# The last two rows of products: one fixed order on TensorE, neighbours in different two-bank tiles, and the last half product in a bank of its own

## The chip, the cores and the metric

The kernel runs on one core of a Trainium2 chip. The metric is device time in microseconds (us); lower is better. The core has five engines that run side by side, each through its own queue in order: TensorE (PE in the profile, with PEld for its weight loads), VectorE (DVE), ScalarE (ACT), GpSimd (POOL) and SyncE (SP), which here only issues transfers. Matrix products land in PSUM, an accumulator memory of eight banks of 128 partitions x 512 float32; everything else that an engine works on lies in SBUF.

## The reference

One layer of a transformer-like block on 512 tokens of 2048 features, in float32:

```python
h = rmsnorm(x, g_attn[l])
proj = h @ w_in[l]                       # q, k, v of 8 + 8 heads, and the forget gates
o_sb, o_fox = stick_breaking_attention(...), forgetting_attention(...)
x = x + concat(head_rmsnorm(o_sb), head_rmsnorm(o_fox)) @ w_out[l]
h2 = rmsnorm(x, g_mlp[l])
u = relu(h2 @ w_up[l])                   # 8192 columns
x = x + (u * u) @ w_down[l]
...
return rmsnorm(x, g_final)               # y, 512 x 2048
```

The change lies wholly in the last two lines: the last part of the product with `w_down`, and the final rmsnorm that needs the sum of squares of a whole row of 2048 values before any of that row can be written.

## The kernel before

Every matrix is split into a high and a low part, and a product is three matmuls (`mm3`, lines 104 to 106: high x high, high x low, low x high). The big products are formed by Strassen-like sums of seven. The product with `w_down` runs over 8192 hidden columns in groups; all but the last four blocks of 128 hidden columns go through the seven-product scheme. The last four blocks are multiplied plainly, by `last_product(t, n, ps)`: `t` is one of four blocks of 128 tokens ("row" t0 to t3), `n` one of four blocks of 512 output columns (n0 to n3). A product (t, n) is 12 matmuls of 128x512 into one PSUM bank: four blocks of hidden columns, three matmuls each. In this document "t2 n3" is such a product. The very last, t3 n3, is made in two halves of 256 columns, which this document calls half a and half b.

After a product, `last_product` issues three more steps. L1240: VectorE adds the PSUM bank onto the running sum `x2(t, n)` in SBUF. L1242: ScalarE squares the result and sums it along the row into `ss3` (two instructions: ACTIVATE and the reading of its accumulator). L1244: GpSimd multiplies the sum by the gain `gf` in place. For the two halves of t3 n3, VectorE does that multiplication itself, into `last_piece` (L1246).

When a row is complete, `last_row(t)` makes the factor of the rmsnorm and scales and stores the row. For t2: L1254 and L1255 (VectorE, mean of the squares), L1265 and L1266 (ScalarE, logarithm and exponential), L1267 and L1268 (VectorE, a Newton step), two scalings of 128x1024 on VectorE (L1276) and two stores (L1277), the first from SyncE's queue and the second from ScalarE's queue. For t3: `mean_square` for the first three squares ahead (L1254, L1255), then L1263 and L1264 once the halves are squared, the same L1265 to L1268, four scalings on VectorE and ScalarE (L1280 to L1284) and four stores (L1286).

PSUM at this stage holds four tiles of two banks each, taken in turn by `two_banks(i)` from three pools: `mps`, `mps2` and two buffers of `dps`. Rows t0 and t1 take one tile for each `n`, with t0 in its first bank and t1 in its second. Rows t2 and t3 take one tile for two neighbouring `n` of the same row: t2 n0 and n1 in one tile, t2 n2 and n3 in the next, t3 n0 and n1, and t3 n2 and n3 in the last. Dependencies between the engines are kept by tile: the first matmul into one bank of a tile waits for VectorE's reading of the other bank if that reading was issued earlier in the program.

In most of the kernel the order on TensorE, ScalarE and VectorE is written out by hand. In this last stage it is not: a scheduler orders the instructions of each engine by its own estimate of times, and `tc.issue_after(ins)` is the means to hold it: instructions of an engine issued inside that block are placed behind `ins` on that engine's queue. It adds no semaphore. In the kernel before, the products of rows t2 and t3 carry no such tie, and the scheduler has put them on TensorE in this order (matmuls in brackets), from t2 n1 on:

```
t2n1 (12)  t2n2 (1)  t1n3 (12)  t2n2 (11)  t3n0 (12)  t3n2 (11)  t2n3 (12)  t3n1 (12)  t3n2 (1)  t3n3 a (12 halves)  t3n3 b (12 halves)
```

Of the kernel before, what the change touches and what calls it, by code (L numbers as in the profile page):

```python
# [16 lines left out]
TB = NT // P  # L17
# [18 lines left out]
def block_kernel(ctx, tc, x, g_attn, w_in, b_f, g_out_sb, g_out_fox, w_out, g_mlp, w_up, w_down, g_final, y):  # L36
# [66 lines left out]
    def mm3(out, sh, sl, mh, ml, first, last):  # L103
        pe.matmul(out, sh, mh, start=first, stop=False, skip_group_check=True)  # L104
        pe.matmul(out, sh, ml, start=False, stop=False, skip_group_check=True)  # L105
        return pe.matmul(out, sl, mh, start=False, stop=last, skip_group_check=True)  # L106
# [59 lines left out]
    with tc.tile_pool(name="att", bufs=1, side="right", reuse_waits="tile") as at:  # L166
# [15 lines left out]
        def accumulate_v(c0, m, steps, prepare=None, more=None, pool_=None):  # L182

            per = NT // m
            banks = [(acc if pool_ is None else pool_).tile([P, NT], F32, tag="acc", name="accv")
                     for _ in range(2 if more is not None else TB // per)]
            if more is not None:
                banks += [more.tile([P, NT], F32, tag="more", name="accm") for _ in range(2)]
            ps = [banks[t // per][:, t % per * m:(t % per + 1) * m] for t in range(TB)]
            k1 = 0  # L190
            for step in steps:
                k0, k1 = k1, k1 + step
                if prepare is not None:
                    prepare(k0, step)
                w = load_w([w_in[k0 * P:(k0 + step) * P, c:c + m // len(c0)].rearrange("(a p) c -> p a c", p=P) for c in c0],
                           step, m)
                for t in range(TB):
                    ts = slice(t * P, (t + 1) * P)
                    for i in range(step):
                        k = k0 + i  # L200
                        mm3(ps[t], hH[k][:, ts], hL[k][:, ts], *w[i], k == 0 and t % per == 0, k == KC - 1)
            return ps
# [126 lines left out]
        def v_columns(h):  # L329
            return 2 * WSB + h * P if h < NH else o0 + 2 * WSB + (h - NH) * P  # L330

        with tc.tile_pool(name="tr0", bufs=2, space=PSUM) as trp:
# [36 lines left out]
            ps = accumulate_v([v_columns(order[0])], 2 * P + NH, [1, 1] + [2] * 7, prepare, trp)  # L369
# [25 lines left out]
        with tc.tile_pool(name="attp", bufs=1, space=PSUM, reuse_waits="tile") as atp:  # L395
# [54 lines left out]
            for n in range(0, 2 * NH, 2):  # L450
# [15 lines left out]
                if n == 2 * NH - 2:  # L466
                    ps = accumulate_v([v_columns(order[n])], 2 * P, [4] * 4, pool_=accs[1])
# [228 lines left out]
    def out_piece(p, db, m0):  # L696

        hi, lo = (w.rearrange("p (a b) -> p a b", a=2) for w in hi_lo(2 * NT))
        if db == 0 and p in (1, 2):
            begun_ = [sp.dma_start(w.bitcast(F32), wraws[p - 1][:, m0 // 2, i]) for i, w in enumerate((hi, lo))][1]  # L700
        elif db == 0 and p == 6:
            begun_ = sp.dma_start(hi.bitcast(F32), whigh[:, m0 // 2])
            sp.dma_start(lo.bitcast(F32), wsums[:, m0 // 2, 3, db])
        else:
            raw = out_weights(p, db, m0)
            casts[0] = split(hi, lo, raw[0])
            begun_ = raw[1]
        ps = {2: B[db], 5: C, 3: C}.get(p, A[db])
        for t in range(2):
            ts = slice(t * P, (t + 1) * P)  # L710
            for i in range(2):
                mm3(ps[:, t, :], G[p][0][:, m0 + i, ts], G[p][1][:, m0 + i, ts], hi[:, i, :], lo[:, i, :],
                    m0 + i == 4 and p in (1, 5, 2), m0 + i == 3)
        return begun_
# [60 lines left out]
    for db in range(2):  # L775
# [25 lines left out]
        for i, p in enumerate(G_ORDER):  # L801
            for m0 in (2,) if db == 0 and p in (1, 2) else (4, 6, 0, 2):
                ins = out_piece(p, db, m0)
# [96 lines left out]
    def x2(t, n):  # L900
        return M[QUADS[t // 2][n // 2]][:, t % 2, n % 2, :]
# [78 lines left out]
    ins = units[0].multiply(1, begun[0])  # L980
# [5 lines left out]
    for p in (1, 2):  # L986
        ins = units[1].product(p)
    left_form(4, 1, 0)
    left_form(5, 1, 0)
    for p in (5, 6, 7, 4, 3):  # L990
        for j in range(2):

            with tc.issue_after(ins.ins):
                ins = units[j].product(p)
# [80 lines left out]
    with tc.manual_schedule(engines={pe.engine, act.engine, dve.engine}):  # L1075
# [5 lines left out]
        for k in range(len(steps)):  # L1081
            n = steps[k][2]
# [45 lines left out]
    ws, us = {}, [None, None]  # L1128
# [28 lines left out]
    bs, srcs, rooms, banks, residual = {(0, 0): b_first}, {}, {}, {}, []  # L1157

    def down_at(k):
        g, db, i, p, u0 = down[k]  # L1160
        return g, db, i, p, u0, min(2, GROUPS[g][1] - u0)

    with tc.manual_schedule(engines={pe.engine, act.engine, dve.engine}):
        for k in range(-4, len(down)):
            g, db, i, p, u0, m = down_at(max(k, 0))
# [35 lines left out]
            n = GROUPS[g][1]  # L1201
# [7 lines left out]
    g, db, i, p = down[-1][:4]  # L1209
# [15 lines left out]
        for o, a, b_ in sums:  # L1225
            dve.tensor_tensor(*(M1[db] if i == 1 else M[i][:, :, db, :] for i in (o, a, b_)), op=ALU.add)

    def last_product(t, n, ps):
        ts = slice(t * P, (t + 1) * P)

        parts = [slice(0, NT)] if (t, n) != (TB - 1, 3) else [slice(0, 2 * P), slice(2 * P, NT)]
        for j, cols in enumerate(parts):
            for i in range(4):
                wh, wl = ws[n, i // 2]
                mm3(ps[:, cols], *(h[:, ts] for h in us[i // 2][i % 2]), wh[:, i % 2, cols], wl[:, i % 2, cols],
                    i == 0 and j == 0, i == 3)
        order_ = ExitStack()
        for j, cols in enumerate(parts):
            x2_ = x2(t, n)[:, cols]
            ins = dve.tensor_tensor(x2_, x2_, ps[:, cols], op=ALU.add)  # L1240
            junk = spare.tile([P, NT], F32, tag="junk", name="junk3")
            act.activation(junk[:, cols], x2_, AF.Square, accum_out=last_sum if j else ss3[:, t, n:n + 1])  # L1242
            if len(parts) == 1:
                pool.tensor_tensor(x2_, x2_, gf[:, n * NT:(n + 1) * NT], op=ALU.mult)  # L1244
            else:
                scaled = dve.tensor_tensor(last_piece[:, cols], x2_, gf[:, n * NT:(n + 1) * NT][:, cols], op=ALU.mult)  # L1246
                order_.enter_context(tc.issue_after(scaled.ins))
        order_.close()
        return ins

    def mean_square(t, tile):

        v, c = tile, 4 if t < TB - 1 else 3
        dve.tensor_reduce(v, ss3[:, t, :c], axis=mybir.AxisListType.X, op=ALU.add)  # L1254
        dve.tensor_scalar(v, v, 1.0 / D, ev[:, t:t + 1], op0=ALU.mult, op1=ALU.add)  # L1255

    def last_row(t):

        v, a, b_ = (cp.tile([P, 1], F32, name=f"{c}3{t}") for c in "vab")
        if t < TB - 1:  # L1260
            mean_square(t, v)
        else:
            dve.tensor_scalar(before_last, ss3[:, t, 3:4], 1.0 / D, before_last, op0=ALU.mult, op1=ALU.add)  # L1263
            dve.tensor_scalar(v, last_sum, 1.0 / D, before_last, op0=ALU.mult, op1=ALU.add)  # L1264
        act.activation(a, v, AF.Ln)  # L1265
        act.activation(a, a, AF.Exp, scale=-0.5)  # L1266
        dve.tensor_scalar(b_, a, v, a, op0=ALU.mult, op1=ALU.mult)  # L1267
        dve.tensor_scalar(v, b_, -3.0, a, op0=ALU.add, op1=ALU.mult)  # L1268
        rows_ = y[t * P:(t + 1) * P]
        if t < TB - 1:  # L1270
            for i, q in enumerate((sp, act)):
                m = M[QUADS[t // 2][i]][:, t % 2]
                if t < 2:
                    act.mul(m, m, v)
                else:
                    dve.tensor_scalar(m, m, v, None, op0=ALU.mult)  # L1276
                q.dma_start(rows_[:, i * 2 * NT:(i + 1) * 2 * NT].rearrange("p (a b) -> p a b", a=2), m)  # L1277
        else:
            m = [x2(t, 0), x2(t, 1), x2(t, 2), last_piece]
            act.mul(m[1], m[1], v)  # L1280
            dve.tensor_scalar(m[3], m[3], v, None, op0=ALU.mult)
            dve.tensor_scalar(m[0], m[0], v, None, op0=ALU.mult)
            act.mul(m[2][:, 2 * P:], m[2][:, 2 * P:], v)
            dve.tensor_scalar(m[2][:, :2 * P], m[2][:, :2 * P], v, None, op0=ALU.mult)  # L1284
            for n, q in ((3, sp), (1, act), (0, sp), (2, act)):
                q.dma_start(rows_[:, n * NT:(n + 1) * NT], m[n])  # L1286
# [18 lines left out]
    def two_banks(i):  # L1305
        return homes[i][0].tile([P, 2, NT], F32, tag=homes[i][1], name="acce")

    for n in range(4):
        two = two_banks(n)
        for t in range(2):  # L1310
            last_product(t, n, two[:, t])
    for db in range(2):
        closing(db, (7, 7, 6), (4, 4, 7), (7, 7, 5))
    for t in range(2):
        last_row(t)
    for t in range(2, TB):
        for n in range(4):
            if n % 2 == 0:
                two = two_banks(2 * (t - 2) + n // 2)
            ins = last_product(t, n, two[:, n % 2])  # L1320
            if (t, n) == (TB - 1, 2):
                mean_square(t, before_last)
        with tc.issue_after(ins.ins):
            last_row(t)
# [29 lines left out]
```

## Time and profile before

| what | value |
|---|---|
| median of 3 runs | 2051.01 us (2050.29 to 2051.45) |
| the profiled execution's own time | 2051.27 us |
| span of the profiled execution, first to last instruction | 2049.5 us |
| granted TensorE clock, mean | 0.999 |
| TensorE busy | 2030.9 us, 99% of the span |
| VectorE / ScalarE / GpSimd busy | 1667.6 / 1093.2 / 57.9 us |
| last matmul of 128x512 starts / last matmul of all ends | 2035.5 / 2040.2 us |

Times in the profile are microseconds from the start of the span. A timeline row gives start, duration, engine, line, operation, output and inputs, shapes, how often; in square brackets stands how long the engine was idle before it and which instruction released it. Consecutive instructions of an engine overlap at their edges, by some tenths of a microsecond. A row of the chain of work that ended last gives the start of a piece, its share of the chain in us, and the instruction.

### The profile page before, as it was taken

What the parts mean: (1) busy time and instruction counts of PE and PEld (TensorE: products, weight loads), DVE (VectorE), ACT (ScalarE), POOL (GpSimd) and SP (SyncE); (2) the same over time, 40 slices, a digit from 0 to 9 for tenths busy, and PEclk for the clock granted to TensorE, in tenths of its full rate; (3) what the DMA queues carried; (4) which work ended last, traced back from release to release, by engine and by line L of the source; (5) the groups of instructions that cost most, each with busy time, mean ns of one, the idle gap of its engine ahead of it and who ended that gap; (6) DMA issues with size and microseconds to landing.
All of it is one profiled execution on the core that took longest, in us unless ns stands there. A gap on an engine that the chain in (4) does not pass through costs nothing.

```text
span 2049.5 us, 26810 instructions
## 1 busy us (share of the span) xinstructions
PE 2030.9 (99%) x10322; PEld 1735.9 (85%) x10322; DVE 1667.6 (81%) x1892; ACT 1093.2 (53%) x1578; POOL 57.9 (3%) x76
## 2 busy tenths in 40 slices
PE   8999999999999999999999999999999999999997
PEld 8888888888888888988888888888888888888886
DVE  5677755566577678899999999998798888888896
ACT  5444433445455566667677676776644344444443
POOL 0000000000010000000000000000000000000004
PEclk9999999999999999999999999999999999999999
DMA  7878743232328882656666667667685674674642
GB/s 242 292 289 269 254 127 90 73 93 75 80 74 276 281 279 90 221 175 190 212 195 208 200 196 221 186 205 256 231 298 202 224 259 171 233 264 170 218 152 82
DMA packets 258848, 402.40 MB, mean 196 GB/s; under 512 B 9456, under 2 KB 154912, under 8 KB 251168
## 3 DMA queue, kind: packets, MB, share of 16 engines
q1 hardware_dynamic: 257760, 398.56, 58.8%
q10 hardware_dynamic: 960, 2.13, 0.3%
q8 instruction: 81, 1.33, 0.3%
q14 instruction: 47, 0.39, 0.1%
HBM read 307.85 MB, written 92.80 MB: 195 GB/s over the span
## 4 chain that ended last, share of the span: by engine, by line
PE 94%; DVE 3%; ACT 1%; DMA 1%; issue 1%; SPq 0%; POOL 0%; ACTq 0%; DVEq 0%
PE psa L594 10%; PE accd L104 8%; PE accd L106 8%; PE accd L105 8%; PE accq L105 6%; PE accq L104 6%; PE accq L106 6%; PE psa L596 5%; PE psc L594 5%; PE psc L596 3%; PE psb L594 3%; PE accv L104 2%; PE accv L105 2%; PE accv L106 2%; PE m L104 1%; PE m L105 1%
## 5 line engine op out<-in xcount | busy, mean ns | idle before, releaser
L1172 ACT CAST wh<-wd 128x1024 fp32r<-128x1024 f32 x126 | 125.0, 999 | 166.3 <-PE accd L106 54.8
L1062 DVE TENSOR_TENSOR wl<-wu,wh 128x1024 fp32r<-128x1024 f32 x157 | 191.4, 1220 | 15.3 <-ACT wh L1056 15.3
L104 PE MATMUL accq<-hH,wh 128*128 128x512 f32 x512 | 200.6, 392 | 0.4 <-DVE vl L75 0.4
L106 PE MATMUL accq<-hH,wl 128*128 128x512 f32 x512 | 200.4, 391 | 0.0
L105 PE MATMUL accq<-hL,wh 128*128 128x512 f32 x512 | 200.3, 391 | 0.0
L594 PE MATMUL psa<-f,wh 128*128 128x512 f32 x728 | 182.5, 393 | 0.3 <-ACT l L628 0.3
L1056 ACT CAST wh<-wu 128x1024 fp32r<-128x1024 f32 x157 | 166.4, 1060 | 28.5 <-issue 11.3
L105 PE MATMUL accd<-wl,uf 128*128 128x512 f32 x436 | 169.8, 389 | 0.0
L106 PE MATMUL accd<-wh,uf 128*128 128x512 f32 x436 | 169.8, 389 | 0.0
L104 PE MATMUL accd<-wh,uf 128*128 128x512 f32 x436 | 169.6, 389 | 0.0
L72 DVE TENSOR_TENSOR wl<-wraw,wh 128x1024 fp32r<-128x1024 f32 (+2 forms) x101 | 119.7, 1186 | 56.5 <-ACT wh L71 50.9
L71 ACT CAST wh<-wraw 128x1024 fp32r<-128x1024 f32 (+2 forms) x101 | 101.8, 1009 | 112.8 <-PE accq L105 69.2
L1179 DVE TENSOR_TENSOR wl<-wd,wh 128x1024 fp32r<-128x1024 f32 x126 | 144.0, 1151 | 13.2 <-ACT wh L1172 12.7
L594 PEld LDWEIGHTS psa<-f,wh 128*128 128x128 f32 x728 | 131.1, 189 | 23.9 <-ACT l L628 0.5
L946 DVE TENSOR_TENSOR m<-m,accd 128x1024 f32<-128x1024 f32 x84 | 102.2, 1217 | 47.7 <-PE accd L106 47.7
L1172 ACT CAST wx<-wd 128x1024 fp32r<-128x1024 f32 (+1 forms) x82 | 80.8, 994 | 110.6 <-PE accd L106 43.6
L104 PEld LDWEIGHTS accq<-hH,wh 128*128 128x128 f32 x512 | 96.2, 188 | 20.1 <-PE accv L106 0.8
L106 PEld LDWEIGHTS accq<-hH,wl 128*128 128x128 f32 x512 | 96.2, 188 | 19.3
L105 PEld LDWEIGHTS accq<-hL,wh 128*128 128x128 f32 x512 | 96.2, 188 | 19.2
L104 PE MATMUL accd<-wx,uf 128*128 128x512 f32 x284 | 110.6, 389 | 0.0
L105 PE MATMUL accd<-wx,uf 128*128 128x512 f32 x284 | 110.6, 389 | 0.0
L106 PE MATMUL accd<-wx,uf 128*128 128x512 f32 x284 | 110.6, 389 | 0.0
(375 smaller groups left out, 4933.0 us busy)
## 6 DMA issues: line engine op xcount, KB each, us to landing
wu<-in_w_up_dram SPq DMA_DIRECT2D x60, 1024.0 KB, 6.5
ufd<-st SPq DMA_DIRECT2D x98, 512.0 KB, 3.9
wd<-in_w_down_dram SPq DMA_DIRECT2D x48, 1024.0 KB, 7.8
wraw<-in_w_in_dram SPq DMA_DIRECT2D x84, 512.0 KB, 3.8
uf<-ufd SPq DMA_DIRECT2D x42, 1024.0 KB, 6.9
mixed<-in_w_out_dram SPq DMA_DIRECT2D x8, 2048.0 KB, 7.7
wsums<-mixed SPq DMA_DIRECT2D x8, 2048.0 KB, 7.3
wo<-wsums SPq DMA_DIRECT2D x28, 512.0 KB, 4.4
```

Source lines behind the costliest of these rows:

```text
L71: ins = act.copy(hi, src)
L72: lows[0] = dve.tensor_tensor(lo, src, hi.bitcast(F32), op=ALU.subtract)
L104: pe.matmul(out, sh, mh, start=first, stop=False, skip_group_check=True)
L105: pe.matmul(out, sh, ml, start=False, stop=False, skip_group_check=True)
L106: return pe.matmul(out, sl, mh, start=False, stop=last, skip_group_check=True)
L594: pe.matmul(ps, hi[:, a, :], f_both(p, a), start=a == PAIRS[0] and p in (1, 5), stop=False, skip_group_check=True)
L596: ins = pe.matmul(ps[:, 2 * P:], lo[:, a, :], f_parts(p, a)[0], start=False, stop=a == PAIRS[-1], skip_group_check=True)
L946: dve.tensor_tensor(M[p][:, :, db, :], M[p][:, :, db, :], ps, op=ALU.add)
L1056: act.copy(rooms[k][0], srcs[k])
L1062: lows[0] = dve.tensor_tensor(lo, srcs.pop(k), hi.bitcast(F32), op=ALU.subtract)
L1172: act.copy(rooms[k + 3][0], srcs[k + 3])
L1179: dve.tensor_tensor(rooms[k + 2][1], srcs.pop(k + 2), rooms[k + 2][0].bitcast(F32), op=ALU.subtract)
```

## The change

It does three things, all in the code for rows t2 and t3.

First, the four PSUM tiles are now taken once, when t = 2, one for each `n`, and shared by the two rows: t2 n in the first bank of tile n, t3 n in the second. Two products that follow each other on TensorE thus lie in different tiles.

Second, the matmuls of each product are placed behind the last matmul of the product before, in the order of the program.

Third, half b of t3 n3 no longer lies in the bank of half a. It goes into the first bank of tile 1, where t2 n1 was. Each half now begins its own accumulation.

```diff
-    def last_product(t, n, ps):
+    def last_product(t, n, *banks):
...
-        for j, cols in enumerate(parts):
+        for ps, cols in zip(banks, parts):
             for i in range(4):
                 wh, wl = ws[n, i // 2]
-                mm3(ps[:, cols], *(h[:, ts] for h in us[i // 2][i % 2]), wh[:, i % 2, cols], wl[:, i % 2, cols],
-                    i == 0 and j == 0, i == 3)
+                mul = mm3(ps[:, cols], *(h[:, ts] for h in us[i // 2][i % 2]), wh[:, i % 2, cols], wl[:, i % 2, cols],
+                          i == 0, i == 3)
         order_ = ExitStack()
-        for j, cols in enumerate(parts):
+        for j, (ps, cols) in enumerate(zip(banks, parts)):
...
-        return ins
+        return mul, ins
...
+    four, mul = [], None
     for t in range(2, TB):
         for n in range(4):
-            if n % 2 == 0:
-                two = two_banks(2 * (t - 2) + n // 2)
-            ins = last_product(t, n, two[:, n % 2])
+            if t == 2:
+                four.append(two_banks(n))
+            banks = [four[n][:, t - 2]] + ([four[1][:, 0]] if (t, n) == (TB - 1, 3) else [])
+            with ExitStack() as order_:
+                if mul is not None:
+                    order_.enter_context(tc.issue_after(mul.ins))
+                mul, ins = last_product(t, n, *banks)
```

The built program differs from the one before only in this stage. The number of instructions is the same on every engine. TensorE's order from t2 n1 on becomes:

```
t2n1 (12)  t1n3 (12)  t2n2 (12)  t2n3 (12)  t3n0 (12)  t3n1 (12)  t3n2 (12)  t3n3 a (12 halves)  t3n3 b (12 halves)
```

VectorE's order, from the addition of t2 n3 on, in the kernel before (upper line, from t3 n0) and after:

```
before: add t3n0, add t2n3, L1254 L1255 L1267 (t2), add t3n1, add t3n2, L1268 (t2), L1276 x2, L1254 L1255 (t3), add a, L1246 a, add b, L1263, L1246 b, L1264 ...
after:  add t2n3, L1254 L1255 L1267 (t2), add t3n0, L1268 (t2), L1276 x2, add t3n1, add t3n2, add a, L1254 (t3), L1246 a, L1255 (t3), add b, L1263, L1246 b, L1264 ...
```

On ScalarE the squares follow those additions; the store of t2's second half (L1277), which waits for the second L1276, stands ahead of the square of t3 n1 in the kernel after, and behind the square of t3 n2 in the kernel before. ScalarE's other L1277 stores move behind one square each. The orders of GpSimd and SyncE are the same.

## The prediction

> **What bounds the kernel now.** I read the page first (busy shares and the chain that ended last), then the chain from 2032 us on, then each engine's timeline of the last 35 us.
>
> ```profile
> PE 2030.9 (99%) x10322; PEld 1735.9 (85%) x10322; DVE 1667.6 (81%) x1892; ACT 1093.2 (53%) x1578; POOL 57.9 (3%) x76
> ...
> PE 94%; DVE 3%; ACT 1%; DMA 1%; issue 1%; SPq 0%; POOL 0%; ACTq 0%; DVEq 0%
> ```
>
> TensorE is the bound, and the edit adds and removes no matmul. What can move is an idle gap of TensorE in the last stage, and what follows its last matmul.
>
> ```profile
> 2016.71 0.39 PE L104 MATMUL acce<-ws,us 128*128 128x512 f32 x1
> ...
> 2035.29 0.61 PE L106 MATMUL acce<-ws,us 128*128 128x512 f32 x2
> 2037.08 0.39 PE L104 MATMUL acce<-ws,us 128*128 128x256 f32 x1 [1.17 <-DVE m L1240]
> 2037.30 0.28 PE L105 MATMUL acce<-ws,us 128*128 128x256 f32 x1
> ...
> 2039.94 0.28 PE L106 MATMUL acce<-ws,us 128*128 128x256 f32 x1
> ```
>
> The first row is the first matmul of t2 n1; the last of the pair at 2035.29, starting at 2035.51, is the 84th behind it and the last of 512 columns. Between them TensorE never waits: 18.80 us / 83 steps = 0.2266 us a step, 2.72 us a product. Then it stands idle for 1.17 us: half a of t3 n3 waits for VectorE's addition of t3 n2, which lies in the same two-bank tile and whose last matmul the scheduler had put directly ahead. The 24 half-width matmuls step by 2.64 us / 22 = 0.120 us and end at 2040.22.
>
> ```profile
> 2033.00 0.70 DVE m L1240
> ...
> 2034.48 0.72 ACT junk L1242 x2
> ...
> 2035.84 1.19 DVE m L1240 x2
> ...
> 2037.26 3.55 DVE m L1276 x2
> ...
> 2040.91 0.21 DVE ss L1255
> 2041.12 0.34 DVE m L1240
> ...
> 2041.90 0.34 DVE m L1240
> ...
> 2042.33 0.52 ACT junk L1242 x2
> ...
> 2044.21 0.72 ACT m L1280
> 2044.93 0.40 ACT m L1283
> ```
>
> The chain leaves TensorE even before that gap: at 2033.00 VectorE adds t2 n3, then come t2's mean and factor, two additions, and the two scalings of row t2 (L1276, 3.55 us, to 2040.81). Only then does VectorE reach the halves of t3 n3, although TensorE was done at 2040.22. The addition of half b ends at 2042.24. From there to the end nothing of the edit plays a part. So two things stand in the way: the gap, and row t2's scalings behind t2 n3, a product multiplied late (after t3 n0 and most of t3 n2).
>
> **The change part by part.** I use the program's order on each engine and the steps above.
>
> (1) TensorE's order and tiles. From t2 n1 at 2016.71 the products start 2.72 us apart: t1 n3 2019.43, t2 n2 2022.15, t2 n3 2024.87, t3 n0 2027.59, t3 n1 2030.31, t3 n2 2033.03, half a 2035.74. An addition on VectorE starts 0.20 us after the next product's start:
>
> ```profile
> 2027.79 0.69 DVE L1240 TENSOR_TENSOR m<-m,acce 128x512 f32<-128x512 f32 x1 [1.41 <-PE acce L106]
> 2026.48 2.17 ACT L1274 ACTIVATE m<-m,v 128x1024 f32<-128x1024 f32 x2
> 2033.72 0.63 ACT L1242 ACTIVATE junk<-m 128x512 f32<-128x512 f32 x1 [5.07 <-DVE m L1240]
> 2034.26 0.18 ACT L1242 ACTIVATION_READ_ACCUMULATOR junk<-m 128x1 f32 x1
> 2034.52 2.52 POOL L1244 TENSOR_TENSOR m<-m,gf 128x512 f32<-128x512 f32 x2 [5.17 <-ACT junk L1242]
> 2044.55 0.48 DVE L1282 TENSOR_SCALAR m<-m,v 128x512 f32<-128x512 f32 x1
> 2044.95 0.35 DVE L1284 TENSOR_SCALAR m<-m,v 128x256 f32<-128x256 f32 x1
> ```
>
> (The first row is t3 n0 before, which ended in the place that t2 n3 has now.) Now the waits of the new tiles. t2 n3 takes the tile of t1 n3: added by 2023.3, needed at 2024.87. t3 n2 shares with t2 n2, added by 2025.8, needed at 2033.03. Half a shares with t2 n3, added by 2028.5, needed at 2035.74: the gap goes, with 7 us to spare. The ties themselves cost nothing: they are places in TensorE's own queue and TensorE had no gap between products. So half a starts at 2035.74, the last matmul at 2035.74 + 23 x 0.120 = 2038.50, and TensorE ends at 2038.78, 1.44 us earlier.
>
> (2) Half b in another tile. It waits for the addition of t3 n1, its tile's other bank, which stands behind the L1276 pair on VectorE. Needed at 2037.18, so I follow row t2. Add t2 n3 2027.79 to 2028.48; ScalarE is busy with L1274 until 2028.65, so the square runs 2028.68 to 2029.40 (0.63 + 0.18, overlapping). From L1254 to the first L1276 it took 2034.48 to 2037.26, 2.78 us, with two additions between; with one (0.6 less) L1276 starts at about 2031.6. GpSimd's part for t2 n3 is over by then (2029.5 + 1.26 = 2030.7). The pair takes between 2 x 0.75 us alone (0.48 for 512, 0.35 for 256 columns: 0.13 per 256, so 0.74 for 1024) and the 3.55 it took beside GpSimd: it ends at 2033.1 to 2035.2, I take 2034.3, since one GpSimd operation (t3 n0) falls beside it and two did before. The addition of t3 n1 ends 0.69 later, 2035.0 (at most 2035.9). Half b finds its bank free. The second bank also lets half a be added while half b is multiplied: before, both additions ran after the last matmul.
>
> (3) The moved store. t2's second store now stands ahead of the square of t3 n1 on ScalarE. Its issue took 0.34 us:
>
> ```profile
> 2040.84 0.34 ACTq L1277 DMA_DIRECT2D out_dram<-m  x1
> 2044.96 0.85 ACTq L1286 DMA_DIRECT2D out_dram<-m  x2
> ...
> out_dram<-m ACTq DMA_DIRECT2D x3, 512.0 KB, 2.7
> ```
>
> It waits for the pair, as the addition of t3 n1 does, and is issued beside that addition: nothing is lost. The other moved ScalarE stores are 0.4 us each in a stage where ScalarE idles; SyncE's and GpSimd's queues keep their order, and t2's stores now go some 6 us earlier and land in 2.7, clear of the last ones.
>
> (4) What is late next. Add t3 n2: 2035.94 to 2036.63, square to 2037.38, GpSimd's t3 n2 from 2037.46 (0.08 after, as at 2034.52) to 2038.72. VectorE: add half a at 2037.07 + 0.28 + 0.04 = 2037.39 to 2037.80, L1254, then L1246 on half a, ready at 2038.0, beside GpSimd. What that does is seen here:
>
> ```profile
> 2003.36 1.22 DVE L1226 TENSOR_TENSOR m<-m,m 128x1024 f32<-128x1024 f32 x1
> 2005.06 3.53 POOL L1244 TENSOR_TENSOR m<-m,gf 128x512 f32<-128x512 f32 x2 [3.30 <-ACT junk L1242]
> 2007.36 2.30 DVE L1226 TENSOR_TENSOR m<-m,m 128x1024 f32<-128x1024 f32 x1
> ...
> 2037.26 2.99 POOL L1244 TENSOR_TENSOR m<-m,gf 128x512 f32<-128x512 f32 x2 [0.22 <-ACT junk L1242]
> ...
> 2041.48 0.42 DVE L1246 TENSOR_TENSOR last<-m,gf 128x256 f32<-128x256 f32 x1
> ```
>
> L1226, of two SBUF operands like L1246, took 1.22 us alone and 2.30 when GpSimd worked until 2008.59: it ended 1.07 after GpSimd, so all but 0.15 of it came after. L1246 then ends at 2038.72 + 0.42 - 0.15 = 2038.99, L1255 0.21 later, and the addition of half b (0.34 on the chain) at 2039.54. The bounds: unhindered, L1246 ends at 2038.4, the addition starts 0.04 after TensorE's end and ends at 2038.82 + 0.41 = 2039.23; with the pair at its full 3.55 us, t3 n1's square ends at 2036.7, GpSimd does t3 n1 and n2 one behind the other (2 x 1.26, and 0.25 each as in the 2.99 row) to 2039.7 and half b is added by 2040.5. The rows lie nearest the middle value.
>
> A rule speaks here. The Trainium skill, "SBUF — State Buffer", section "Who interferes with whom", says that VectorE with two SBUF inputs and GpSimd reading SBUF take a shared port in turn and that the second "fully blocks". By it L1246 would run whole behind GpSimd, to 2039.14, and the saving would be 2.55 instead of 2.70 us. The 2.30 row agrees within 0.15 us.
>
> Sum: half b's addition ends at 2039.54 instead of 2042.24, 2.70 us earlier; square, L1264 to L1268, scalings and stores follow at the same distances. The profiled run took 2051.27 us (span 2049.5, 1.77 around it): 2048.57. It stands 0.26 above the median of 2051.01, so against the median 2048.3. The case's own range is 1.7 to 3.0 us saved, 2048.0 to 2049.3, and some 0.6 for the spread of runs (2050.29 to 2051.45) on either side.
>
> **The rivals.** *Only the gap is won.* If VectorE still reaches half b as late after TensorE's end as now (2042.24 - 2040.22 = 2.02 us; forecast 0.76), the saving is TensorE's 1.44 us: 2049.6. For it: L1276 or GpSimd work that falls later than I place it. Against: the pair starts 5.7 us earlier.
>
> *Slower: the L1276 pair holds half b.* Half b waits for an addition queued behind row t2's scalings, a wait that the kernel before did not have. From the pair's end through add, square, two GpSimd operations, L1246 and half b's addition it is 0.69 + 0.75 + 0.08 + 2.52 + 0.27 + 0.55 = 4.9 us; the saving is gone when the pair ends after 2037.4, and the kernel is over 0.2% (4.1 us) slower after 2041.5: 2055.2. That needs t2's factor 6 us later than worked out, for instance ScalarE held by a store that waits for an earlier one to land (2.7 us each). Against: t2's mean needs one square, and ScalarE is free from 2028.65.
>
> *It does nothing.* If the end hung on the last stores alone: 2051.0. Against: they are issued at 2044.96, when L1283 is nearly through, and earlier stores have landed.
>
> *Faster by over 0.2%.* 1.4 us more than the sum, 2046.9 or less: the last stores, now alone in the queues, would have to land sooner as well. Their burst already starts at once; little speaks for it.
>
> **How the numbers follow.** Case by the sum (2048.3) 0.78; only the gap (2049.6) 0.08; nothing (2051.0) 0.04; slower (2055.2) 0.04; faster (2046.9) 0.06. 0.2% is 4.1 us, about what a measurement of this kernel can tell from no change: faster takes the last case and a little of the first's lower edge, 0.1; slower 0.05; within 0.2% the rest, 0.85. The range goes from 2047.2 (3.0 saved, and runs low) to 2050.6, which takes in the gap-only case with the runs' spread.
>
> **What the profile would show.** Right: no idle time of TensorE before the first 256-column matmul; last matmul ending near 2038.8; L1276 near 2031.6, before the addition of t3 n1; half b added by 2039.5; GpSimd's t3 n2 ending just before L1246. Wrong: a wait on L1240 at the first matmul of half b, a chain through L1276 again, or GpSimd's two last operations back to back after 2036.5.

## The result and the profile after

The changed kernel takes 2048.24 us (median of 22 runs, 2047.04 to 2049.67) where the kernel before takes 2050.94 (22 runs, 2049.46 to 2053.24): 2.70 us less. The ratio is 0.9987, with a 95% interval of 0.9981 to 0.9993. So the gain is clear of no change, though it is smaller than the 0.2% at which the prediction drew its line.

The page of the changed kernel, busy shares and the chain that ended last:

```profile
PE 2030.4 (99%) x10322; PEld 1734.8 (85%) x10322; DVE 1666.6 (81%) x1892; ACT 1093.2 (53%) x1578; POOL 57.5 (3%) x76
...
PE 94%; DVE 4%; ACT 1%; issue 1%; DMA 1%; POOL 0%; SPq 0%; ACTq 0%; DVEq 0%
```

The shares say nothing new, as is to be expected when 2.7 us of 2050 are at stake. The profiled execution has a span of 2045.7 us, 3.8 less than that of before, and 2.7 of these are the stage's. To see this, both traces need a common mark. Up to the matmuls of t1 n2 the two programs are the same, so VectorE's addition of t1 n2 serves; in the kernel before:

```profile
2016.91 0.69 DVE L1240 TENSOR_TENSOR m<-m,acce 128x512 f32<-128x512 f32 x1 [2.03 <-PE acce L106]
```

and VectorE's timeline of the changed kernel, with its rows of this stage that matter:

```profile
2015.76 0.69 DVE L1240 TENSOR_TENSOR m<-m,acce 128x512 f32<-128x512 f32 x1 [2.03 <-PE acce L106]
...
2030.28 2.45 DVE L1276 TENSOR_SCALAR m<-m,v 128x1024 f32<-128x1024 f32 x2
2032.65 0.68 DVE L1240 TENSOR_TENSOR m<-m,acce 128x512 f32<-128x512 f32 x1
...
2036.69 1.27 DVE L1246 TENSOR_TENSOR last<-m,gf 128x256 f32<-128x256 f32 x1
...
2038.01 0.41 DVE L1240 TENSOR_TENSOR m<-m,acce 128x256 f32<-128x256 f32 x1
```

The mark lies at 2016.91 and at 2015.76: this execution was 1.15 us ahead before the change could act. From here on, times "after the mark" are times less that of the mark in the same trace. From the mark to the end of the span it is 2049.5 - 2016.91 = 32.59 us before and 2045.7 - 2015.76 = 29.94 us after: 2.65 us less, and this agrees with the medians. TensorE and GpSimd in the changed kernel:

```profile
2034.60 0.28 PE L104 MATMUL acce<-ws,us 128*128 128x256 f32 x1
...
2037.35 0.28 PE L106 MATMUL acce<-ws,us 128*128 128x256 f32 x1
```

```profile
2036.38 1.29 POOL L1244 TENSOR_TENSOR m<-m,gf 128x512 f32<-128x512 f32 x1 [0.88 <-ACT junk L1242]
```

The first half-width matmul has no idle time in front of it any more (before: 1.17 us). Row t2's two scalings start 14.52 us after the mark instead of 20.35, and take 2.45 us instead of 3.55. And the chain that ended last, which left TensorE ahead of the gap before, now follows TensorE through half a of t3 n3, and then half a's gain beside GpSimd:

```profile
2036.23 0.42 DVE m L1240
...
2036.72 1.24 DVE last L1246
2037.96 0.12 DVE ss L1255
2038.08 0.34 DVE m L1240
...
2038.51 0.52 ACT junk L1242 x2
...
2040.38 0.72 ACT m L1280
2041.11 0.40 ACT m L1283
```

The tail behind half b's addition is as long as before: from 2038.42 to 2045.7 it is 7.28 us, before from 2042.24 to 2049.5 7.26.

### The profile page after: what moved, and what is told of

Its sections match the earlier page's. It is cut to its first block, busy times and chain, and to the rows that moved or that the text cites. A ratio compares the mean times of both kernels' runs of the same rounds, so it can differ in the third digit from the quotient of the medians.

```text
span 2045.7 us, 26813 instructions
## 1 busy us (share of the span) xinstructions
PE 2030.4 (99%) x10322; PEld 1734.8 (85%) x10322; DVE 1666.6 (81%) x1892; ACT 1093.2 (53%) x1578; POOL 57.5 (3%) x76
## 4 chain that ended last, share of the span: by engine, by line
PE 94%; DVE 4%; ACT 1%; issue 1%; DMA 1%; POOL 0%; SPq 0%; ACTq 0%; DVEq 0%
PE psa L594 10%; PE accd L104 8%; PE accd L105 8%; PE accd L106 8%; PE accq L104 6%; PE accq L105 6%; PE accq L106 6%; PE psa L596 5%; PE psc L594 5%; PE psc L596 3%; PE psb L594 3%; PE accv L104 2%; PE accv L105 2%; PE accv L106 2%; PE m L104 1%; PE m L105 1%
```

## The experiments

The medians of single kernels here are of 10 or 11 runs each and carry an interval of some 0.09% (1.8 us) on either side, too wide for terms of 0.3 us. The time from the mark to the span's end is free of what happens ahead of the stage. In a second profile of the changed kernel it came out within 0.02 us; every other kernel was profiled once. So each verdict below rests on that time ("the stage"), and the ratio is given beside it.

| kernel | stage, us | against before | TensorE ends | half b added | ratio of medians, 95% interval |
|---|---|---|---|---|---|
| before | 32.59 | | 23.31 | 25.32 | |
| changed | 29.94 | -2.65 | 21.87 | 22.66 | 0.9987 (0.9981 to 0.9993) |
| changed, once more | 29.96 | -2.63 | 21.87 | 22.66 | 0.9986 (0.9977 to 0.9994) |
| ties alone | 33.65 | +1.06 | 25.07 | 26.31 | 1.0007 (0.9998 to 1.0016) |
| tiles and half b's bank alone | 30.79 | -1.80 | 21.87 | 23.42 | 0.9992 (0.9984 to 1.0001) |
| changed, both halves in one bank | 30.45 | -2.14 | 21.87 | 23.11 | 0.9987 (0.9978 to 0.9996) |
| before, t3 n3 in another tile | 32.38 | -0.21 | 21.87 | 25.05 | 1.0000 (0.9991 to 1.0009) |
| changed, halves' gains behind half b | 29.67 | -2.92 | 21.88 | 22.33 | 0.9986 (0.9977 to 0.9995) |
| changed, no gain of t3 n2 | 29.63 | -2.96 | 21.87 | 22.33 | 0.9989 (0.9980 to 0.9997) |
| changed, 4 more scalings | 30.54 | -2.05 | 21.87 | 22.90 | 0.9991 (0.9982 to 1.0000) |
| changed, wait before half a put back | 30.66 | -1.93 | 22.92 | 23.37 | 0.9990 (0.9981 to 1.0000) |
| changed, 8 more scalings | 33.24 | +0.65 | 25.20 | 25.66 | 1.0003 (0.9993 to 1.0012) |

The columns "TensorE ends" and "half b added" are times after the mark; the latter is the end of that addition's row.

### The order alone

```diff
...
-            banks = [four[n][:, t - 2]] + ([four[1][:, 0]] if (t, n) == (TB - 1, 3) else [])
+            if n % 2 == 0:
+                two = two_banks(2 * (t - 2) + n // 2)
...
-                mul, ins = last_product(t, n, *banks)
+                mul, ins = last_product(t, n, *[two[:, n % 2]] * 2)
```

> The products of rows t2 and t3 in one fixed order, but with the old tiles (two neighbours n of one row share a tile) and both halves of t3 n3 in one bank. Theory (the order brings row t2's scalings forward, and the separate tiles take away one wait per pair): three neighbours now follow each other in one tile (t2 n2 and n3, t3 n0 and n1, t3 n2 and n3), each costing TensorE about 1.0 us of idle time (an addition of 0.69 us plus its start, less the step of 0.23). TensorE ends some 2.9 us later than in the changed kernel, the additions of the halves run after it, and the addition of half b ends about 0.6 us later than in the kernel before: 0.3 to 1.0 us slower than before. Rival (the ties alone carry the gain): 1.3 to 2.7 us faster than before.

1.06 us slower in the stage, a little more than the 0.3 to 1.0 expected: TensorE ends 3.20 us later than in the changed kernel, where 2.9 was expected. TensorE's timeline, all its rows of the stage with idle time:

```profile
2027.45 0.50 PE L104 MATMUL acce<-ws,us 128*128 128x512 f32 x1 [0.78 <-DVE m L1240]
2033.96 0.50 PE L104 MATMUL acce<-ws,us 128*128 128x512 f32 x1 [0.78 <-DVE m L1240]
2040.48 0.39 PE L104 MATMUL acce<-ws,us 128*128 128x256 f32 x1 [0.78 <-DVE m L1240]
```

One wait per pair of neighbours, as the theory has it, and the rival falls. Half a starts 21.93 us after the mark against 18.84 in the changed kernel, so a wait costs 1.03 us. The order is no gain of its own. It is paid for with three waits unless the neighbours lie in different tiles. The scheduler's mixed order in the kernel before had only one such wait, of 1.17 us.

### The tiles alone

```diff
-            with ExitStack() as order_:
-                if mul is not None:
-                    order_.enter_context(tc.issue_after(mul.ins))
-                mul, ins = last_product(t, n, *banks)
+            mul, ins = last_product(t, n, *banks)
```

> The new tiles and the separate bank for half b, but no ties: the scheduler then puts t2 n3 one product (12 matmuls, 2.72 us) later on TensorE than the changed kernel does, with t3 n0 ahead of it. Theory: no idle time of TensorE before half a, but row t2's scalings start about 2.7 us later than in the changed kernel, t3 n2's addition waits behind them, and half b is added 0.8 to 1.2 us later: 1.4 to 1.9 us faster than before, where the full change gives 2.7. Rival (tiles alone do it): the full 2.7 us.

1.80 us faster than before, as expected, and 0.85 short of the full change. TensorE ends where it ends in the changed kernel. VectorE's timeline shows what is missing:

```profile
2034.87 2.66 DVE L1276 TENSOR_SCALAR m<-m,v 128x1024 f32<-128x1024 f32 x2
...
2039.05 1.52 DVE L1246 TENSOR_TENSOR last<-m,gf 128x256 f32<-128x256 f32 x1
```

The scalings start 17.26 us after the mark (2034.87 - 2017.61) instead of 14.52: 2.74 us later, one product of 2.72, because without ties the scheduler puts t3 n0 ahead of t2 n3. The additions of t3 n1 and n2 follow the scalings, GpSimd comes to t3 n2 later, and half a's gain beside it ends 22.96 us after the mark instead of 22.20. So the ties are worth 0.85 us, once the tiles are there.

### Half b's bank

```diff
-            banks = [four[n][:, t - 2]] + ([four[1][:, 0]] if (t, n) == (TB - 1, 3) else [])
+            banks = [four[n][:, t - 2]] * 2
...
-                          i == 0, i == 3)
+                          i == 0 and j == 0, i == 3)
```

> The changed kernel with half b back in the bank of half a. Theory: TensorE as in the changed kernel, but the addition of half a waits for the last matmul of half b, so that half a's addition, its gain (0.42 us) and half b's addition stand one behind the other after TensorE's end: half b is added 1.1 us after 38.8 on the scale of the prediction, 0.4 us later than in the changed kernel: 2.3 us faster than before. Rival (the separate bank is what counts): most of the 2.7 us is gone.

2.14 us faster than before, where 2.3 was expected; the separate bank is worth 0.51 us, a fifth of the gain and not most of it, as the rival had it. Half a's addition waits for the last matmul of half b:

```profile
2038.56 0.42 DVE L1240 TENSOR_TENSOR m<-m,acce 128x256 f32<-128x256 f32 x1 [0.93 <-PE acce L106]
2039.01 0.43 DVE L1246 TENSOR_TENSOR last<-m,gf 128x256 f32<-128x256 f32 x1
2039.35 0.41 DVE L1240 TENSOR_TENSOR m<-m,acce 128x256 f32<-128x256 f32 x1
```

### The gap alone, in the old order

```diff
-            ins = last_product(t, n, two[:, n % 2])
+                if (t, n) == (2, 2):
+                    other = two
+            ins = last_product(t, n, two[:, n % 2] if (t, n) != (TB - 1, 3) else other[:, 0])
```

> The kernel before, with t3 n3 alone moved to another tile (that of t2 n2 and n3), in the old order. TensorE's idle 1.2 us before half a goes and TensorE ends 1.4 us earlier. Theory: nothing is gained (0 to 0.2 us), because row t2's scalings still stand in front of the halves' additions on VectorE, ending where they ended. Rival (only the gap is won): 1.4 us faster.

TensorE ends 1.44 us earlier, and the stage is only 0.21 us shorter, as expected. VectorE's timeline:

```profile
2038.17 3.52 DVE L1276 TENSOR_SCALAR m<-m,v 128x1024 f32<-128x1024 f32 x2
2041.61 0.14 DVE L1254 TENSOR_REDUCE ss<-ss 128x1 f32<-128x3 f32 x1
2041.67 0.40 DVE L1240 TENSOR_TENSOR m<-m,acce 128x256 f32<-128x256 f32 x1
```

The scalings end where they ended before (23.87 us after the mark, before 23.90), and half a's addition stands behind them. TensorE's idle time, the wait that catches the eye, was not what set the end.

### The gap alone, in the new order

```diff
-            banks = [four[n][:, t - 2]] + ([four[1][:, 0]] if (t, n) == (TB - 1, 3) else [])
+            banks = [four[n][:, t - 2]] if (t, n) != (TB - 1, 3) else [four[2][:, 0], four[1][:, 0]]
```

Half b's matmuls are tied behind half a's as well, so that the scheduler keeps the halves' order.

> The changed kernel with half a of t3 n3 put back beside t3 n2, into the first bank of its tile, so that the wait for t3 n2's addition returns; order, ties and half b's bank as in the changed kernel. Theory: TensorE waits 1.0 us before half a, as each of the three pairs did with the ties alone, and here it reaches the end: half b is added 0.7 to 0.9 us later than in the changed kernel (0.3 of the 1.0 is hidden behind half a's gain and GpSimd), 1.8 to 2.0 us faster than before. Rival (the gap is worth as little as in the old order): 0.2 us.

```profile
2037.63 0.39 PE L104 MATMUL acce<-ws,us 128*128 128x256 f32 x1 [0.78 <-DVE m L1243]
```

The wait is back with the 0.78 us of the ties alone. TensorE ends 1.05 us later and the stage is 0.72 us longer than in the changed kernel, both as expected. So the wait before half a is worth 0.21 us behind the scalings (1.17 us of idle time) and 0.72 where they are out of the way (0.78 us).

### Half a's gain and GpSimd

Two kernels ask what the new chain hangs on. In the first, the two gains (L1246) leave `last_product` and stand behind the addition of half b:

```diff
-                scaled = dve.tensor_tensor(last_piece[:, cols], x2_, gf[:, n * NT:(n + 1) * NT][:, cols], op=ALU.mult)
-                order_.enter_context(tc.issue_after(scaled.ins))
...
+            scaled = gain(slice(0, 2 * P))
+            with tc.issue_after(scaled.ins):
+                ins = dve.tensor_scalar(v, last_sum, 1.0 / D, before_last, op0=ALU.mult, op1=ALU.add)
+            with tc.issue_after(ins.ins):
+                gain(slice(2 * P, NT))
```

> The changed kernel with the gains of the two halves (the multiplications into last_piece) moved behind the addition of half b: half a's gain just ahead of the row's mean, half b's behind it, in the time in which VectorE waits for the logarithm and exponential. Theory (after the change, half b's addition is late because half a's gain waits for GpSimd's t3 n2): half b is added 0.04 us after TensorE's end, and the end comes 0.3 to 0.4 us earlier than in the changed kernel: 3.0 to 3.1 us faster than before. Rival (TensorE's end decides): no difference to the changed kernel.

In the second, GpSimd does not multiply t3 n2 by its gain:

```diff
-            if len(parts) == 1:
+            if len(parts) == 1 and (t, n) == (TB - 1, 2):
+                pass
+            elif len(parts) == 1:
                 pool.tensor_tensor(x2_, x2_, gf[:, n * NT:(n + 1) * NT], op=ALU.mult)
```

> The changed kernel without GpSimd's multiplication of t3 n2 by the gain: that quarter of the last row stays without its gain. Theory: half a's gain on VectorE takes its 0.42 us alone instead of 1.27, half b's addition starts with TensorE's end, and the end comes 0.3 us earlier than in the changed kernel. Rival (the long time of that operation has another cause, such as its own wait for half a's square): 1.27 us again, and no difference.

VectorE's timeline of the first, half b's addition:

```profile
2038.74 0.42 DVE L1240 TENSOR_TENSOR m<-m,acce 128x256 f32<-128x256 f32 x1 [0.70 <-PE acce L106]
```

and of the second, half a's gain:

```profile
2038.30 0.42 DVE L1248 TENSOR_TENSOR last<-m,gf 128x256 f32<-128x256 f32 x1
```

Both add half b 22.33 us after the mark, 0.33 earlier than the changed kernel, and shorten the stage by 0.27 us (0.3 to 0.4 expected) and 0.31 us (0.3 expected). In the first VectorE waits for TensorE; in the second the gain takes 0.42 us instead of 1.27. So GpSimd's multiplication of t3 n2 beside half a's gain costs the changed kernel 0.3 us. The first kernel leaves nothing out, and among those that don't its stage is the shortest, 2.92 us under that of before. Its median, beside the changed kernel's on the same chip, doesn't show the 0.27 us (2047.91 and 2047.53).

### The slack behind the scalings

```diff
                     dve.tensor_scalar(m, m, v, None, op0=ALU.mult)
+                    for _ in range(2):
+                        late.append(dve.tensor_scalar(m, m, 1.0, None, op0=ALU.mult))
```

Together with ties that keep all of them ahead of t3 n1's addition. The second kernel has `range(4)`, and ties that keep the additions of t3 n1, n2 and n3 in this order.

> The changed kernel with each of row t2's two scalings followed by two more by 1.0, all six ahead of the addition of t3 n1 on VectorE: some 2.8 us more work there (4 x 0.7). Theory (between the scalings' end and half b's addition lies a chain of 4.9 us through t3 n1's addition, square and two operations of GpSimd; in the changed kernel it has slack, since t3 n2 is multiplied later): the scalings end at 36.7 on the scale of the prediction, half b is added near 41.6, about 2.0 us later than in the changed kernel; 0.6 us faster than before. Rival (slack to spare): no change to the changed kernel. Rival (they hold half b itself and everything behind it in full): 2.8 us later, no gain left.

> The changed kernel with each of row t2's scalings followed by four more by 1.0, all ahead of t3 n1's addition: 4.8 us more than in the changed kernel (2.4 for half as many), so that they end 21.8 us after the addition of t1 n2 starts. Theory (the slack is used up; half a's gain slips in between two operations of GpSimd, so only one of them counts): TensorE waits about 2.2 us before half b for t3 n1's addition, half a's gain ends 0.28 us after GpSimd's t3 n1, and half b is added near 25.3 us after that start, where the kernel before has it at 25.3 as well: no gain left (within 0.5 us). Rival (the slope stays as small as with half as many): 0.3 us more than there.

With four more, VectorE and GpSimd:

```profile
2033.55 2.49 DVE L1280 TENSOR_SCALAR m<-m 128x1024 f32<-128x1024 f32 x4
2035.96 1.60 DVE L1240 TENSOR_TENSOR m<-m,acce 128x512 f32<-128x512 f32 x3
...
2037.53 2.70 POOL L1244 TENSOR_TENSOR m<-m,gf 128x512 f32<-128x512 f32 x2 [4.45 <-ACT junk L1242]
...
2038.31 0.79 DVE L1246 TENSOR_TENSOR last<-m,gf 128x256 f32<-128x256 f32 x1
...
2039.60 0.90 DVE L1246 TENSOR_TENSOR last<-m,gf 128x256 f32<-128x256 f32 x1
2040.47 0.21 DVE L1266 TENSOR_SCALAR v<-ss 128x1 f32<-128x1 f32 x1
```

(Two added lines of code make L1264 of the other kernels L1266 here.) The scalings end 2.41 us later than in the changed kernel, 19.38 after the mark. Half b is added only 0.24 us later, and the stage is 0.60 longer. Neither 2.0 nor 2.8 nor nothing: the expectation failed. It had half a's gain wait for both of GpSimd's operations. The timeline shows it going in after the first of the two. Seen one by one, GpSimd's operations take 1.29 us from 2037.53 to 2038.82 and 1.45 us from 2038.78 to 2040.23; half a's gain ends at 2039.10, 0.28 us after the first. The other 0.36 us arise behind half b's addition. There the second operation counts after all: half b's gain beside it takes 0.90 us instead of 0.41, to 2040.50, and L1264, which stands behind that gain on VectorE, starts only as it ends. ScalarE's square is late as well: it starts 0.37 us after the addition's end instead of 0.09, and its sum is read out by 2040.44. What holds the square I did not find, but in this kernel an earlier one would not have brought L1264 forward.

With eight more, the scalings end 21.78 us after the mark, and TensorE waits:

```profile
2039.40 0.42 PE L104 MATMUL acce<-ws,us 128*128 128x256 f32 x1 [2.01 <-DVE m L1240]
2039.62 0.41 PE L105 MATMUL acce<-ws,us 128*128 128x256 f32 x1
```

Half b waits for t3 n1's addition, as the prediction's slower rival had it. Half a's gain ends 0.28 us after GpSimd's first operation, and half b is added 25.66 us after the mark, where 25.3 was expected. No gain is left, as expected, but the loss of 0.65 us is more than the 0.5 allowed for. Some 0.3 us of it arise behind half b's addition, where ScalarE's square again starts 0.38 us after the addition's end. The 0.36 us of the addition are TensorE's. Its steps after the wait are 0.21 us instead of 0.12; the table of stretches shows a lower granted clock (columns: stretch, busy times by engine, granted clock, DMA share, GB/s):

```profile
2039.40:2040.40 1.00, 1.00 (x5) 1.00 (x6) 0.97 (x3) 0.93 (x3) 0.16 (x1) 0.60 1.03 418
2040.40:2041.40 1.00, 1.00 (x7) 1.00 (x6) 1.00 (x1) 0.97 (x4) 1.00 (x1) 0.50 1.03 426
```

## Why the prediction was right

The forecast was 2048.3 us; 2048.24 was measured. That the two agree to 0.06 us is luck, since the interval of the medians runs from 1.4 to 3.9 us saved; what bears the forecast out is the stage and the steps in it. Step by step, with the prediction's times less its own mark of 2016.91:

- **TensorE's order and tiles.** Half a was to start at 18.83 and TensorE to end at 21.87 after the mark; measured 18.84 and 21.87. The wait is gone, and TensorE shows no other.
- **Row t2's scalings.** Forecast start 14.7, end 17.4; measured 14.52 and 16.97. The pair took 2.45 us, between the bounds of 1.5 and 3.55, a little under the 2.7 taken. The lower bound was set too high: the four scalings by 1.0 in the kernel with four more, with GpSimd idle, took 2.49 us, 0.62 each. None of this was on the path that ended last.
- **Half b in another bank.** Half b did not wait for t3 n1's addition (over at 17.6, needed at 20.3). The experiment with one bank puts a price of 0.51 us on this part, which the prediction had not worked out by itself.
- **What is late next.** Half a's gain was to end at 22.08, slowed by GpSimd; it ended at 22.20, 0.29 us after GpSimd (forecast 0.27). The addition behind it followed by 0.46 us instead of the 0.55 summed, so that two errors of about 0.1 us nearly cancel. The bound without GpSimd, 0.31 us better, is what the kernel without that multiplication measured (0.31). The Trainium skill's rule of a full block ("SBUF — State Buffer", "SBUF: two separate sides") would have the gain run whole, 0.42 us, after GpSimd's end; the rows here leave 0.27 to 0.29, so all but some 0.13 us of it comes after, at ends of GpSimd's rows that are rough.
- **The sum.** Half b's addition was to end 2.70 us earlier; it ended 2.66 us earlier, and the stage is 2.65 us shorter.
- **The rivals.** "Only the gap is won" fell: half b is added 0.79 us after TensorE's end (forecast 0.76), not 2.02 as before, and the gap alone brought 0.21 us. It had TensorE's 1.44 us as its price, but in the old order the scalings hid nearly all of it. "It does nothing" fell with the result. "The scalings hold half b" is a real mechanism, as the kernel with eight more shows, but the changed kernel is far from it. "Faster by over 0.2%" fell with the result.

One piece of the rival of the scalings was wrong: the chain of 4.9 us from the scalings' end to half b's addition, and with it the point (scalings ending at 2037.4, or 20.5 after the mark) from which the gain would be gone. It counted both of GpSimd's operations, and the trace shows half a's gain going between them. At 19.4 the stage still was 2.05 us shorter than before, at 21.8 it was 0.65 us longer; the point lies between these and was not measured more closely. In the forecast itself this chain served only for the lower end of its range, 1.7 us saved with a pair at its full length, and that end was not reached. A slip in the working changes nothing: the matmul at 2035.51 is the 83rd behind the first, not the 84th, and the sum does use 83.

How the 2.65 us are made up, as the experiments cut them: tiles and half b's bank without ties 1.80, the ties on top 0.85. The separate bank accounts for 0.51 us, and the missing wait before half a for 0.72, each taken out of the changed kernel alone; the parts overlap and do not add up to the whole.

## What to carry to other kernels

Idle time of the bounding engine is worth what the chain behind it leaves of it: a wait of 1.17 us before the last product cost 0.21 us while VectorE was late anyway, and one of 0.78 us cost 0.72 us when it was not. When a row's normalisation is queued on the same engine as the next row's additions, look at which product completes that row and multiply it early. A fixed order needs accumulators that neighbours do not share: the order without the tiles was 1.06 us slower than the scheduler's mixture, while the tiles without the order already brought 1.80 of the 2.65 us.

## What was not expected of the hardware

After 2.01 us without a matmul (the kernel with eight more scalings) TensorE's granted clock was halved for nearly all of the 12 matmuls that were left: 0.60 over the first microsecond, 0.50 from then on, with steps of 0.21 us instead of 0.12. After 1.17 us (the kernel before) only the first step was longer (0.22 us) and the granted clock read 1.00 throughout. So a wait can cost more than its length: half b started 2.16 us later than in the changed kernel and ended 3.33 later. The Trainium skill, "TensorE: Matmul & The Clock Gate", section "What's actually happening", names about 3.4 us of idleness for this; the trace shows it at 2.0.

The length of the wait alone does not seem to decide. The clock fell 0.2 us after this wait was over. In the other eleven traces it fell behind the last matmul of all, after anything from 2.4 us (tiles and half b's bank alone) to 5.0 us (before, t3 n3 in another tile). In the twelve traces the full clock is on record for either 2030.93 or 2034.34 us, 3.41 us apart, as if it could change only at steps of that length. In the 3.41 us ahead of the fall TensorE worked for 1.4 us here and for at most 1.0 us in the other traces; 1.9 us of work in such a stretch (before, t3 n3 in another tile) left the clock up. By these figures it would be the work within a fixed stretch that counts, and where a wait lies would matter as much as its length. No run was made to test this.

The spread of whole runs comes from far ahead of this stage: the mark lies between 2015.04 and 2018.55 us in the eleven profiles other than that of before, in programs that are the same up to there. By the 2000th of 10322 matmuls, some 410 us into the span, each of these traces is as far ahead of that of before, or behind it, as it is at the mark, to within 0.3 us. The stage of the changed kernel, the one that was profiled twice, repeats to 0.02 us.
